# Hybrid decoder layer on one core: the small stores of the softmax statistics move from SP's queue to POOL's

## The chip, the cores and the metric

The kernel runs on one NeuronCore of a Trainium2 chip. The core has a matmul engine (PE), a vector engine (DVE), an activation engine (ACT), a general engine (POOL) and a sequencer that here only issues DMA transfers (SP). Each engine works through its own list of instructions in order; semaphores tie the lists together. The metric is device time in microseconds for one launch, the median of several runs.

## The reference

One layer of a decoder trunk, sequence 2048, width 1024, float32. After an RMS norm and one input projection, four mixers of 256 channels run side by side; their gated outputs are concatenated, projected, normed and added to the input. The change touches mixer A, softmax attention with three dilated windows, whose outputs are mixed by their softmax denominators:

```python
def _dilated_branch(q, k, v, window, dil, slopes):
    ...
    scores = jnp.where(mask, scores + bias, -jnp.inf)
    m = jnp.max(scores, axis=-1, keepdims=True)
    p = jnp.exp(scores - m)
    den = jnp.sum(p, axis=-1, keepdims=True)
    o = jnp.einsum('bhrnqk,bhrnkd->bhrnqd', (p / den).astype(v.dtype), vc)
    lse = (m + jnp.log(den))[..., 0]
    ...

def _dilated_mixture(q, k, v):
    slopes = _alibi_slopes(q.shape[1])
    outs, lses = [], []
    for window, dil in DILATED_PAIRS:          # ((128, 1), (512, 4), (2048, 16))
        o, lse = _dilated_branch(q, k, v, window, dil, slopes)
        outs.append(o)
        lses.append(lse)
    w = jax.nn.softmax(jnp.stack(lses), axis=0)
    o = jnp.einsum('gbhs,gbhsd->bhsd', w.astype(v.dtype), jnp.stack(outs))
    ...
```

There are four heads of 64 channels, 2048 queries each. Mixers B (spatial gating), C (pooling) and D (retention) are computed earlier and are not touched.

## The kernel before

Matmul operands are split into a high and a low part of float32r, so that one product is several matmuls.

**Stages.** First come the projections and the mixers B, C and D, in two halves of the sequence; they leave q, k, v and the gates in device memory (`qk`, `vd`, `agd`, `yb`). Then follows attention, head by head: heads 0 and 1 in `attention(0)`, 2 and 3 in `attention(1)`. Each head runs its branches in the order of dilation 4, 16, 1. A branch has 16 blocks of 128 queries, so a head has 48 blocks and the stage 192. For each block PE makes scores (`ps_s`), DVE adds the bias and takes the maximum (`att_p`, L639), ACT the exponential (L641), PE transposes (`ps_pt`), ACT and DVE split (L648, L649), PE multiplies by the values (`ps_o`), and ACT and DVE add the two halves into `att_o` (L663, L664).

**The loads of a head** are q2 (L565, L566), k2a (L568), k2b (L569) and three sets of values `att_v` (L578, L581, L576). They share seven buffers with the reordered queries `q2b` (L589 on DVE and POOL, L591 on DVE), so that each load waits until the last reader of an earlier tile is done.

**The statistics.** Each branch leaves maximum and denominator of its queries in `att_st`, 128 x 2 x 16. `keep_stats` transposes them on PE (`ps_st`), copies them on DVE to `sT` (L724, one buffer for all branches) and stores `sT` to `std` in device memory in the order of the sequence: eight stores of 2 KB for dilation 4 (L732), two for dilation 16 (L735), one for dilation 1 (L726). They are 40 stores and 4 more over the stage. `weigh` loads a head's three branches back (`sv`, L740), works out the weights on DVE (L742 to L752) and stores them to `fd` (L753).

**Combining.** `combine(0)` takes heads 0 and 1 in eight chunks of 256 queries, and has two buffers, so the chunks go in pairs. A chunk loads the weights `fb` (L763) and the gate `sga` (L765); POOL multiplies two branches (L766, L767), DVE the third (L768), adds (L769, L770) and gates (L772); ACT and POOL split the result (L776, L777), and SP stores it (L779). It has no place of its own in time: it runs among the blocks of heads 2 and 3. `combine(1)` follows the last head.

**Partial and final output.** Nine of the 16 output tiles get the products of mixers B, C and D during attention (`partial`: load `yraw` L785, split on POOL L797 and L798, matmuls `ps_out`, store `partd` L818). `final` adds attention's part, norms and stores.

**Order.** The code is not run in the order in which it is written: a scheduler orders the instructions of each engine ahead of time, by its own estimate of when each will be ready. Before the change SP issues every DMA. A DMA takes one of eight completion semaphores in turn, so it also waits for the DMA eight places before it.

Of the kernel before, what the change touches and what calls it, by code (L numbers as in the profile page):

```python
# [85 lines left out]
def hymba(ctx: ExitStack, tc: tile.TileContext, x, pre_g, w_in, sgu_g, sgu_w, sgu_b, pool_w,  # L86
          pool_scale, ret_g, w_out, post_g, cmix, catt, out, dbg=None, npart=9, spread=(0.3, 0.95)):
    nc = tc.nc
    V, A, G, T, D = nc.vector, nc.scalar, nc.gpsimd, nc.tensor, nc.sync
# [7 lines left out]
    def transpose(o, i, n=P):  # L97
        T.transpose(o, i, ident[:n, :n])  # L98
# [456 lines left out]
    def attention(p, tab):  # L555
        o01 = (big if p == 0 else po).tile([P, 2, SEQ], F32, tag="big" if p == 0 else "o01", name="att_o01")
        o = [o01[:, 0], o01[:, 1], po.tile([P, SEQ], F32, tag="o2", name="att_o2")]
        for s in range(2):
# [11 lines left out]
            for b, dil in enumerate(DILS):  # L570
                vt = pm.tile([P, 16, 2 * HD], F32R, tag="m8", bufs=7, name="att_v")
                dst = r32(vt)
                if dil == 1:
                    src = v_d[h].rearrange("(n t c) d -> c t n d", c=4, t=32)
                    for c in range(4):
                        D.dma_start(dst[c * 32:(c + 1) * 32], src[c])  # L576
                elif dil == 4:
                    D.dma_start(dst.rearrange("q (j c) d -> q j (c d)", j=4),  # L578
                                v_d[h].rearrange("(j q c) d -> q j (c d)", j=4, c=4))
                else:  # L580
                    D.dma_start(dst.rearrange("q r d -> q (r d)"), v_d[h].rearrange("(q r) d -> q (r d)", r=16))  # L581
                qb = q2
                if dil != 1:
                    qb = pm.tile([P, SEQ], F32R, tag="m8", bufs=7, name="q2b")
                    if dil == 4:
                        src = r32(q2).rearrange("p (j k c i) -> p c j k i", j=4, c=4, i=8)
                        dst = qb.rearrange("p (j c k i) -> p c j k i", j=4, c=4, i=8)
                        for c in range(4):
                            (V if c < 3 else G).tensor_copy(dst[:, c], src[:, c])  # L589
                    else:  # L590
                        V.tensor_copy(qb.rearrange("p (r w i) -> p r w i", r=16, i=8),  # L591
                                      r32(q2).rearrange("p (w r i) -> p r w i", r=16, i=8))
                st = p2.tile([P, 2, 16], F32, tag="stat", bufs=2, name="att_st")
                branch(h, dil, qb, k2a, k2b, vt, tab, o[b], st)
                keep_stats(h, b, dil, st)
# [123 lines left out]
    def keep_stats(h, b, dil, st):  # L719

        pt = ps2.tile([P, GRP], F32, tag="t", bufs=N_T, name="ps_st")
        transpose(pt[:32, :P], st.rearrange("p z n -> p (z n)"))
        sT = p2.tile([32, P], F32, tag="sT", bufs=1, name="sT")
        V.tensor_copy(sT, pt[:32, :P])  # L724
        if dil == 1:
            D.dma_start(st_d[h][b].rearrange("z (n q) -> (z n) q", q=P), sT)  # L726
            return
        for z in range(2):
            dst, src = st_d[h][b, z], sT[z * 16:(z + 1) * 16]
            if dil == 4:  # L730
                for j in range(4):
                    D.dma_start(dst.rearrange("(j k c i) -> j c k i", j=4, k=16, c=4)[j],  # L732
                                src[j * 4:j * 4 + 4].rearrange("c (k i) -> c k i", i=8))
            else:
                D.dma_start(dst.rearrange("(w r i) -> r w i", r=16, i=8), src.rearrange("r (w i) -> r w i", i=8))  # L735

    def weigh(h):

# [175 lines left out]
```

## Time and profile before

| | |
|---|---|
| median of 3 runs | 1062.74 us (1060.38 to 1069.5) |
| profiled execution, its time | 1066.84 us |
| its span, first to last instruction | 1065.1 us |
| its mean granted TensorE clock | 0.973 |
| PE busy | 993.5 us, 93% |
| DVE, ACT, POOL busy | 51%, 36%, 18% |
| DMA | 135.27 MB, 119962 packets |

The profile is one execution. A share of busy time is an average over stages with different limits. A row of a timeline has the start in us, the duration, the engine (SPq is SP's list of DMA issues), the line in the kernel, the operation, what it writes and reads, how many instructions were merged and, in brackets, how long the engine had stood idle before it and what ended that. A row of a group has busy time, mean duration in ns, then the idle time before its instructions and what ended it.

### The profile page before, as it was taken

To read this page: it belongs to the slowest core of one execution; us is meant where nothing else is said; L and a number is where in the kernel's file an instruction comes from. 1 tells how busy PE (TensorE), PEld (TensorE's weight loads), DVE (VectorE), ACT (ScalarE), POOL (GpSimd) and SP (SyncE) were. 2 spreads that over 40 slices of the span, in tenths; PEclk is the share of its full clock that TensorE was granted. 3 is DMA by queue.
4 is the path that set the end of the run, shared out by engine and by line. 5 is a ranking of instruction groups with operands and counts; after the bars stand their busy time and mean duration, and the time that the engine had idled before them with its cause. 6 is when DMAs were issued, how large, how long until landed. Compare 5 with 4: busy or idle time off the path is not lost. (4 is left out here: it accounts for less than half of the span.)

```text
span 1065.1 us, 15690 instructions
## 1 busy us (share of the span) xinstructions
PE 993.5 (93%) x5916; PEld 855.0 (80%) x5916; DVE 540.4 (51%) x1547; ACT 379.6 (36%) x851; POOL 190.9 (18%) x195
## 2 busy tenths in 40 slices
PE   5899999999999999999999999979998779988993
PEld 5888898988877988989898787778988569867872
DVE  7611216696332422023763321287776677547898
ACT  6320222131222421122211121498877448513231
POOL 2310012211232000002210134031122351142000
PEclk9999999999999999999999999998999879989997
DMA  8530313233223331042211830395659953484776
GB/s 279 147 99 20 100 60 114 85 120 92 86 79 99 99 100 39 25 135 80 80 41 50 210 119 20 116 213 162 147 168 201 207 152 85 109 270 129 268 259 217
DMA packets 119962, 135.27 MB, mean 127 GB/s; under 512 B 14928, under 2 KB 95952, under 8 KB 117840
## 3 DMA queue, kind: packets, MB, share of 16 engines
q1 hardware_dynamic: 119888, 134.29, 43.6%
q8 instruction: 46, 0.75, 0.3%
q14 instruction: 28, 0.23, 0.1%
HBM read 97.80 MB, written 36.47 MB: 126 GB/s over the span
## 5 line engine op out<-in xcount | busy, mean ns | idle before, releaser
L95 PE MATMUL ps_t<-hh,w 128*128 128x512 f32 x1152 | 370.1, 398 | 2.3 <-DVE b_t L370 2.3
L95 PEld LDWEIGHTS ps_t<-hh,w 128*128 128x128 f32 x1152 | 216.7, 189 | 52.4 <-issue 3.4
L95 PE MATMUL ps_t<-hl,w 128*128 128x512 f32 x576 | 227.6, 395 | 0.0
L95 PE MATMUL ps_m<-w,hh 128*128 128x256 f32 x1024 | 183.8, 282 | 2.0 <-ACT hh L230 1.6
L95 PE MATMUL ps_out<-wo,yt 128*128 128x512 f32 x576 | 155.6, 414 | 6.1 <-DVE yt L798 3.1
L95 PEld LDWEIGHTS ps_m<-w,hh 128*128 128x128 f32 x1024 | 157.5, 190 | 3.9 <-ACT hh L230 2.8
L95 PE MATMUL ps_m<-w,hl 128*128 128x256 f32 x512 | 145.4, 284 | 0.2 <-DVE hl L231 0.2
L95 PEld LDWEIGHTS ps_out<-wo,yt 128*128 128x128 f32 x576 | 109.8, 198 | 31.1 <-DVE yt L798 4.4
L95 PEld LDWEIGHTS ps_t<-hl,w 128*128 128x128 f32 x576 | 108.7, 189 | 24.3 <-issue 1.4
L250 DVE TENSOR_TENSOR w<-raw,w 128x1024 fp32r<-128x1024 f32 x42 | 59.0, 1412 | 109.6 <-ACT w L248 109.4
L95 PEld LDWEIGHTS ps_m<-w,hl 128*128 128x128 f32 x512 | 97.6, 191 | 0.8 <-DVE hl L231 0.4
L641 ACT ACTIVATE att_p<-att_p,att_st 128x128 f32<-128x128 f32 (+1 forms) x192 | 86.4, 453 | 20.5 <-DVE att_st L639 20.0
L248 ACT ACTIVATE w<-raw 128x1024 fp32r<-128x1024 f32 (+1 forms) x56 | 55.0, 997 | 70.1 <-PE ps_t L95 37.6
L639 DVE CUSTOM_DVE_ANT_0 att_p<-ps_s,tab 128x128 f32<-128x128 f32 (+1 forms) x192 | 60.3, 357 | 34.5 <-PE ps_s L95 31.0
L95 PE MATMUL ps_o<-pt_hi,att_v 128*128 128x128 f32 (+1 forms) x204 | 54.4, 287 | 6.2 <-DVE att_o L664 4.2
L649 DVE TENSOR_TENSOR pt_lo<-ps_pt,pt_hi 128x512 fp32r<-128x512 f32 x80 | 51.2, 650 | 12.5 <-ACT pt_hi L648 12.1
L95 PE MATMUL ps_o<-pt_lo,att_v 128*128 128x128 f32 (+1 forms) x204 | 52.8, 294 | 3.5 <-DVE pt_lo L649 3.4
L98 PE MATMUL ps_pt<-ident,att_p 128*128 128x128 f32 x300 | 51.2, 283 | 0.8 <-ACT att_p L641 0.8
L95 PEld LDWEIGHTS ps_o<-pt_hi,att_v 128*128 128x128 f32 x204 | 40.8, 200 | 9.5 <-DVE att_o L664 4.6
L648 ACT ACTIVATE pt_hi<-ps_pt 128x512 fp32r<-128x512 f32 x80 | 44.1, 563 | 11.2 <-PE ps_pt L98 5.7
L95 PE MATMUL ps_s<-k2a,q2b 128*128 128x128 f32 (+1 forms) x128 | 37.5, 325 | 8.6 <-DMA k2a<-qk 4.4
L95 PEld LDWEIGHTS ps_o<-pt_lo,att_v 128*128 128x128 f32 x204 | 40.6, 199 | 5.9 <-DVE pt_lo L649 4.8
(160 smaller groups left out, 1319.8 us busy)
## 6 DMA issues: line engine op xcount, KB each, us to landing
raw<-in_w_in_dram SPq DMA_DIRECT2D x52, 512.0 KB
qk<-qk_s SPq DMA_DIRECT2D x16, 512.0 KB
att_v<-vd SPq DMA_DIRECT2D x8, 1024.0 KB
xr<-in_x_dram SPq DMA_DIRECT2D x16, 512.0 KB
out_dram<-z SPq DMA_DIRECT2D x15, 512.0 KB
xt<-in_x_dram SPq DMA_DIRECT2D x7, 1024.0 KB
yraw<-yb SPq DMA_DIRECT2D x16, 384.0 KB
partd<-z SPq DMA_DIRECT2D x9, 512.0 KB
```

The costliest lines, as they stand in the source:

```text
L95: return T.matmul(o, lhsT, rhs, start=start, stop=stop, skip_group_check=True)
L98: T.transpose(o, i, ident[:n, :n])
L248: A.activation(hi, raw[:, :, cs], AF.Copy, scale=sc)
L250: eng.tensor_tensor(lo, raw[:, :, cs], r32(hi), ALU.subtract)
L639: V.tensor_tensor_reduce(out=pr[:, u, :w], in0=ps[:, u, :w], in1=bb, scale=-SLOPES[h] * HD ** -0.5, scalar=3e38, op0=ALU.add, op1=ALU.min, ...
L641: A.activation(pr[:, u, :w], pr[:, u, :w], AF.Exp, bias=neg, scale=-1.0, accum_out=st[:, 1, n:n + 1])
L648: A.activation(hi, pt[:, :w], AF.Copy)
L649: V.tensor_tensor(lo, pt[:, :w], r32(hi), ALU.subtract)
```

## The change

The stores of the two dilated branches (L732 and L735) are issued by POOL instead of SP. The store of dilation 1 (L726) stays with SP. The data, their places and their sizes are the same.

```diff
             dst, src = st_d[h][b, z], sT[z * 16:(z + 1) * 16]
             if dil == 4:
                 for j in range(4):
-                    D.dma_start(dst.rearrange("(j k c i) -> j c k i", j=4, k=16, c=4)[j],
+                    G.dma_start(dst.rearrange("(j k c i) -> j c k i", j=4, k=16, c=4)[j],
                                 src[j * 4:j * 4 + 4].rearrange("c (k i) -> c k i", i=8))
             else:
-                D.dma_start(dst.rearrange("(w r i) -> r w i", r=16, i=8), src.rearrange("r (w i) -> r w i", i=8))
+                G.dma_start(dst.rearrange("(w r i) -> r w i", r=16, i=8), src.rearrange("r (w i) -> r w i", i=8))
```

`D` is SP, `G` is POOL. The scheduler makes a new order from it, on every engine, from the end of head 0 on. Three places matter here.

SP where head 1's loads are issued (`q_6493` is head 1's q2, `std_82` head 0's statistics); a row with - stood there before, one with + stands there now:

```order
 L566 DMA q_6493<-qk_66 64x2048
 L548 DMA wo_raw<-in_w_out_dram 128x1024 x2
-L732 DMA std_82<-sT 4x16x8 x8
 L568 DMA k2a<-qk_68 64x2048 x2
-L735 DMA std_82<-sT 16x16x8 x2
 L569 DMA k2b<-qk_68 64x2048 x2
 L578 DMA att_v<-vd 128x4x512
```

The ten stores no longer stand before k2a and k2b. On POOL they stand between the two products of a weight split (L550) and head 1's quarter of `q2b` (L589).

POOL where the first pair of chunks of heads 0 and 1 is combined, while head 2 runs (`std_84` is head 2's statistics, `att_o_5880` and `att_o_5881` the outputs of heads 0 and 1). Before:

```order
L766 TENSOR_TENSOR fb<-fb,att_o_5880 128x256
L767 TENSOR_TENSOR fb<-fb,att_o_5881 128x256
L797 CAST yt<-yraw 128x3x128
L777 TENSOR_TENSOR ysa<-fb,ysa 128x256 x2
L798 TENSOR_TENSOR yt<-yraw,yt 128x3x128
```

And now:

```order
L766 TENSOR_TENSOR fb<-fb,att_o_5880 128x256
L767 TENSOR_TENSOR fb<-fb,att_o_5881 128x256
L797 CAST yt<-yraw 128x3x128
L732 DMA std_84<-sT 4x16x8 x8
L798 TENSOR_TENSOR yt<-yraw,yt 128x3x128
L777 TENSOR_TENSOR ysa<-fb,ysa 128x256 x2
L797 CAST yt<-yraw 128x3x128
L735 DMA std_84<-sT 16x16x8 x2
L798 TENSOR_TENSOR yt<-yraw,yt 128x3x128
```

Eight stores and one L798 have come between the products and L777, and two stores ahead of the next pair. On DVE, 22 score blocks (L639) now stand between L772 of the first pair and L768 of the second, where 8 stood. The three pieces of head 3's `q2b` (L589), which stood in the third pair, now stand in the second.

DVE at the fourth pair, where head 3 begins its values (`att_o_7252` is head 2's output, whose L664 frees a bank for `ps_o`). Before, the pair and the weights of head 2 (L742 to L745) were mixed with L664:

```order
L768 TENSOR_TENSOR fb<-fb,att_o_5880 128x256
L742 TENSOR_TENSOR nm<-sv 128x16
L772 TENSOR_TENSOR fb<-fb,sga 128x2x16x8
L769 TENSOR_TENSOR fb<-fb 128x256
L743 TENSOR_TENSOR nm<-nm,sv 128x16
L664 TENSOR_TENSOR att_o_7252<-ps_o,att_o_7252 64x512
L770 TENSOR_TENSOR fb<-fb 128x256
L745 TENSOR_TENSOR df<-sv,nm 128x48
```

Now L664 follows the whole pair, and the weights precede it:

```order
L752 TENSOR_TENSOR ew<-ew,nm 128x48
L768 TENSOR_TENSOR fb<-fb,att_o_5880 128x256 x2
L769 TENSOR_TENSOR fb<-fb 128x256
L770 TENSOR_TENSOR fb<-fb 128x256
L772 TENSOR_TENSOR fb<-fb,sga 128x2x16x8
L769 TENSOR_TENSOR fb<-fb 128x256
L770 TENSOR_TENSOR fb<-fb 128x256
L772 TENSOR_TENSOR fb<-fb,sga 128x2x16x8
L664 TENSOR_TENSOR att_o_7252<-ps_o,att_o_7252 64x512 x2
```

On PE, 18 `ps_out` now stand ahead of head 3's first `ps_o` where none stood; between that `ps_o` and the last `ps_st` of head 3 there are 19 more than before, and so 37 fewer partial products behind the last `ps_st`. On SP, the last `partd` store and the last two `wo_raw` loads now come before the second `combine` loads its weights of head 3.

## The prediction

> **What bounds the kernel now.** I read the page's head and busy shares first, then the windows, then the timelines of the engines where the small stores stand.
>
> ```profile
> span 1065.1 us, 15690 instructions
> PE 993.5 (93%) x5916; PEld 855.0 (80%) x5916; DVE 540.4 (51%) x1547; ACT 379.6 (36%) x851; POOL 190.9 (18%) x195
> q1 hardware_dynamic: 119888, 134.29, 43.6%
> 450.00:500.00 50.00, 50.00 (x332) 44.12 (x331) 13.56 (x20) 12.24 (x14) 7.58 (x6) 1.00 0.33 103
> 715.00:720.00 5.00, 2.40 (x12) 2.43 (x13) 2.48 (x5) 4.70 (x17) 0.00 (x0) 0.66 1.07 225
> 720.00:725.00 5.00, 3.13 (x15) 2.76 (x15) 1.28 (x6) 3.48 (x7) 0.00 (x0) 0.50 0.83 241
> 850.00:855.00 5.00, 1.84 (x6) 1.12 (x6) 4.02 (x10) 1.29 (x5) 3.98 (x5) 0.50 0.95 377
> ```
>
> A window row gives the stretch, its length, the busy time of PE, PEld, DVE, ACT and POOL, the granted clock, the DMA share and GB/s. The projections fill PE wholly (the row at 450 us), and nothing of the change stands there. The attention stage, from 683 us, has holes on PE: at 715 us, where head 1 begins, and around 850 us, where heads 0 and 1 are combined. In both the granted clock falls to 0.50. So the change is judged at these two places and at what follows them. The data of all DMA goes through one queue, q1, which is SP's; POOL issues none.
>
> **Head 1's start.** On SP the stores stand in front of the loads of the next head (start, duration, issue, count).
>
> ```profile
> L732 SPq DMA_DIRECT2D std<-sT x32: 241/317/855, 702.4 to 896.6; - x32
> 702.41 7.61 SPq L732 DMA_DIRECT2D std<-sT  x8
> 710.12 1.09 SPq L568 DMA_DIRECT2D k2a<-qk  x2
> 712.74 1.09 SPq L569 DMA_DIRECT2D k2b<-qk  x2
> 756.10 9.12 SPq L732 DMA_DIRECT2D std<-sT  x8
> 768.92 0.81 SPq L735 DMA_DIRECT2D std<-sT  x2
> 894.06 2.81 SPq L732 DMA_DIRECT2D std<-sT  x8
> 903.55 1.13 SPq L735 DMA_DIRECT2D std<-sT  x2
> 701.68 0.27 PE L95 MATMUL ps_o<-pt_lo,att_v 128*128 128x128 f32 x1
> 711.69 0.28 PE L95 MATMUL ps_s<-k2b,q 128*128 128x256 f32 x1
> 717.60 0.77 PE L95 MATMUL ps_s<-k2a,q2b 128*128 128x128 f32 x2 [4.42 <-DMA k2a<-qk]
> 722.71 0.44 PE L95 MATMUL ps_s<-k2b,q2b 128*128 128x128 f32 x1 [1.87 <-DMA k2b<-qk]
> ```
>
> Eight L732 stores hold SP for 7.61 us, 0.95 us each, though one issue's median is 0.317 us. Behind them wait k2a and k2b, 1 MB each. I infer that k2a takes the buffer of head 0's first values, last read at 701.68, and k2b one whose last scores run at 711.69. With the stores gone, k2a can go out at about 702 and land by 710, from its own 7.5 us (710.12 to 717.60). k2b is held by PE's read more than by SP: it goes out at about 711.9 instead of 712.74. Its 10 us to landing had k2a ahead in the queue; alone, 1 MB at the window's 225 GB/s is 4.4 us, and with some 2.8 us for issue and latency (estimate, the landing of a small store below) it lands at 719 instead of 722.7. That is 3.7 us. PE meanwhile works through its k2a part and eight ps_o, so its hole is short, and I count 1.3 us for the half-speed clock after it: **-5 us**.
>
> POOL could undo it: its L735 waits for the second transpose sT, and its quarter of q2b (L589) for head 1 stands behind L735.
>
> ```profile
> 696.73 4.75 POOL L550 TENSOR_TENSOR wo<-wo_raw,wo 128x1024 fp32r<-128x1024 f32 x2 [0.60 <-ACT wo L549]
> 711.53 0.28 DVE L724 COPY sT<-ps_st 32x128 f32<-32x128 f32 x1 [0.56 <-PE ps_o L95]
> 712.04 0.61 POOL L589 CAST q2b<-q 128x512 fp32r<-128x512 f32 x1 [10.55 <-PE ps_s L95]
> 786.71 2.78 DMA std<-sT
> ```
>
> **The unknown price** is what one store costs POOL, since no row shows POOL issuing a DMA. From below, an issue on SP, 0.32 us; an instruction that POOL did not have can give it nothing back, so below nothing is excluded. From above, POOL's longest row, L550, 4.75 us for two, so 2.4 us. I take 0.95 us, the pace of these very stores at 702.41, the nearest row.
>
> The Trainium skill, "DMA: Bandwidth & Descriptors", section "Anatomy of one DMA — SWDGE (gpsimd) path", fits about 2.0 us for each DMA on POOL's path, most of it completion and not setup. Were all of the 2.0 us POOL's own time, the sum would end some 30 us higher; if only the setup is, it stands. No run before the change shows which.
>
> At 0.95 us, POOL's eight end at 710 and have landed at 712.8 (2.78 us, the row of L726's store). DVE's second sT copy needs that, as sT has one buffer: DVE stands about 1 us, and all behind it on DVE too. L735 then ends at 715 and L589 at 716, ahead of k2b at 719, which hides them; from 1.4 us a store on it does not. Further on, the stores of the two branches are 12.8 us apart in head 1 (756.10 to 768.92) and 9.5 in head 3; the eight need 7.6 + 2.8 = 10.4, so DVE waits 1 us in head 3. I leave these 2 us inside the roundings.
>
> **The combining of heads 0 and 1** is a chain of four pairs of chunks, each begun by its fb loads.
>
> ```profile
> L768 DVE TENSOR_TENSOR fb<-fb,att_o 128x256 f32<-128x256 f32 x8 | 4.2, 530 | 17.6 <-DMA fb<-fd 17.6
> 810.00 0.42 DVE L768 TENSOR_TENSOR fb<-fb,att_o 128x256 f32<-128x256 f32 x1 [4.85 <-DMA fb<-fd]
> 828.07 0.43 DVE L768 TENSOR_TENSOR fb<-fb,att_o 128x256 f32<-128x256 f32 x1 [3.80 <-DMA fb<-fd]
> 846.21 0.43 DVE L768 TENSOR_TENSOR fb<-fb,att_o 128x256 f32<-128x256 f32 x1 [4.97 <-DMA fb<-fd]
> 866.09 0.43 DVE L768 TENSOR_TENSOR fb<-fb,att_o 128x256 f32<-128x256 f32 x1 [2.84 <-DMA fb<-fd]
> 872.11 0.68 DVE L664 TENSOR_TENSOR att_o<-ps_o,att_o 64x512 f32<-64x512 f32 x1
> 874.90 0.57 DVE L772 TENSOR_TENSOR fb<-fb,sga 128x256 f32<-128x256 f32 x1
> 818.16 0.27 DVE L639 CUSTOM_DVE_ANT_0 att_p<-ps_s,tab 128x128 f32<-128x128 f32 x1
> 823.85 0.41 DVE L639 CUSTOM_DVE_ANT_0 att_p<-ps_s,tab 128x256 f32<-128x256 f32 x1
> 817.92 1.70 POOL L777 TENSOR_TENSOR ysa<-fb,ysa 128x256 fp32r<-128x256 f32 x2 [0.34 <-ACT ysa L776]
> 820.76 3.33 SPq L763 DMA_DIRECT2D fb<-fd  x3
> 842.21 1.17 SPq L578 DMA_DIRECT2D att_v<-vd  x1
> 864.90 4.48 PE L95 MATMUL ps_out<-wo,yt 128*128 128x512 f32 x18 [0.57 <-ACT z L817]
> ```
>
> The pairs begin at 810, 828, 846 and 866 us. DVE stands at the head of each until fb lands, 17.6 us over the stage, and the last product ends at 875.5. In the new order POOL has head 2's eight L732 and an L798 between the products and L777 of pair 1. L777 feeds SP's L779, behind which stand three fb loads, k2b and the values of head 3. The eight cost 7.6 and the L798 1.0 us, so L777 comes at 826.5 instead of 817.9. SP is then otherwise idle, and its three loads, 3.33 us here among q2's and k2a's transfers, should land some 2.5 us sooner: **pair 2** at 834. That wait is filled: 22 score blocks now stand between L772 of pair 1 and L768 of pair 2 where 8 stood, and those 8 (818.16 to 823.85) took 6 us, so 22 take 17. Head 2's two L735, at the head of POOL's products, add 1.9. **Pair 3** follows after 18.1 us as before and 2 us for the three q2b copies that moved into pair 2: 856. Pair 3 then needs 16 us, not 19.9, since the head 3 values that went out at 842 (from 842.21, 2 MB) no longer meet its loads: **pair 4** at 872 to 873, its end at 879. DVE's L664, which frees the bank for head 3's first ps_o, stood inside pair 4 and now stands behind it: 880.5 instead of 872.1, **+8 us**.
>
> **Head 3 and the tail.** In PE's new order 18 ps_out stand ahead of that ps_o, hidden in its wait. 19 more than before stand between it and the last ps_st; at 4.48/18 = 0.25 us, **+4.7 us**. All 37 used to follow the last ps_st.
>
> ```profile
> 920.42 0.11 PE ps_st L98
> 935.86 10.48 DMA partd<-z
> 930.00:940.00 10.00, 7.13 (x21) 5.07 (x21) 2.87 (x2) 2.37 (x4) 2.36 (x1) 0.75 1.05 314
> 1050.00:1060.00 10.00, 0.00 (x0) 0.00 (x0) 9.79 (x31) 1.89 (x5) 0.00 (x0) 0.56 0.55 210
> ```
>
> So PE has 37 x 0.25 = 9.2 us less in the tail. But the tail begins with the second combine, whose fb loads stood behind the last partd store, and ends on DVE, with no matmul after 1050. The last partd and wo_raw, 1 MB, now go out ahead of it, 3.3 us at 314 GB/s. I take **-4 us**, between 0 (the chain alone decides) and -9.2 (PE alone).
>
> **Sum**, against the profiled execution: -5 + 8 + 4.7 - 4 = +3.7 us on 1066.84, of which its span is 1065.1. The median of the runs, 1062.74, lies 0.4% under that execution; I put the same difference on the median: 1066.5 us.
>
> **Rivals.**
>
> *POOL pays much more per store* (slower). For: POOL's plain instructions take 0.5 to 2.4 us. Against: it is busy 18% and could spare the time elsewhere. The point is 1.3 us a store. At 1.6 us: pair 2 another 5.2 us late; head 1's eight landed at 718, L589 done at 722, so 4.5 of the -5 us go; DVE's second copies wait 2.8 more in head 1 and 6 in head 3: 1066.5 + 18.5 = 1085. At 2.4 us, some 1110.
>
> *SP's relief is worth more than POOL's delay* (faster). At 0.32 us a store L777 slips by 3.6, not 8.6 (-5). If the blocks ahead of pair 2 also save its 3.80 us stall (-4) and the tail follows PE (-5), it is 1052. For: all 17.6 us of stalls end on fb loads that SP issues. Against: the chain is serial, and work that fills a wait does not shorten it.
>
> *No more than a new order*: the stores cost neither queue anything that shows, and the same matmuls run in another order. 1063, inside the forecast's own range.
>
> **How the numbers follow.** Forecast, with the third case in it: 0.49 (1057 to 1075). POOL's price: 0.30, half of it over 1085. SP's relief: 0.21. This kernel's measurement cannot tell less than 1%, 1052 to 1073, from no change. Faster 0.19, nearly all from the relief; slower 0.31, the price and the forecast's edge; same 0.50. The range, 1049 to 1086, takes in the relief and a price up to 1.6 us, and leaves the dearer half of the price out.
>
> **What will show it.** 40 issues by POOL, whose spacing is the price: 0.95 us. k2a out at 702, head 1's first k2b scores at 719. L777 of pair 1 some 9 us behind its L776. The last product of pair 4 at 874 to 880, the last ps_st at about 928, then a shorter tail. I am wrong if POOL spends over 1.3 us a store, if DVE's second sT copies stand over 2 us, or if the tail shrinks by the full 9 us.

## The result and the profile after

The changed kernel takes 1072.67 us (median of 9 runs, 1068.69 to 1076.88), the kernel before, run beside it, 1064.10 us (9 runs). The ratio is 1.0072, 95% interval 1.0049 to 1.0095: slower by 0.7%, where the forecast had 0.35%, inside its range and its case of "no change". (A ratio with its interval is worked out from all runs of both kernels; it is not the quotient of the two medians, which here is 1.0081.) Its profiled execution took 1068.69 us.

First the page of the changed kernel: span, busy times, then the DMA queues with packets, MB and share of 16 engines.

```profile
span 1067.0 us, 15740 instructions
PE 989.6 (93%) x5916; PEld 852.5 (80%) x5916; DVE 537.3 (50%) x1547; ACT 379.9 (36%) x851; POOL 212.0 (20%) x235
q1 hardware_dynamic: 115536, 134.16, 43.5%
q0 software_dynamic: 1280, 0.16, 0.2%
```

POOL now has a queue of its own, q0, with 40 more instructions and 21 us more busy time. PE has the same 5916 matmuls, and its busy time is 3.9 us less; what grew is its idle time.

The two profiled executions can't be laid over each other by their clocks. The last L331 on ACT ends the stage ahead of attention; here are its rows, of before, then of after.

```profile
683.42 1.10 ACT L331 ACTIVATE ag_s<-ps_t 128x512 f32<-128x512 f32 x1 [4.31 <-PE ps_t L95]
679.01 1.10 ACT L331 ACTIVATE ag_s<-ps_t 128x512 f32<-128x512 f32 x1 [4.31 <-PE ps_t L95]
```

The execution of before came there 4.41 us later, in a stage that the change does not touch. All positions below are therefore counted from this row in each kernel's own trace ("at 28.1" is 28.1 us behind it). From there before needs 381.7 us to its end and after 388.0: **+6.3**, while the spans differ by 1.9.

**Head 1's start.** Timelines of SP, POOL, DVE and PE after, then POOL's issues of a store and the time from issue to landing of all transfers of `std`, then the DMA share (the column ahead of the GB/s) by 5 us. The last three rows are what SP waited for ahead of k2a, the time to landing of k2a's two halves, and PE's first scores on k2b.

```profile
701.10 1.09 SPq L568 DMA_DIRECT2D k2a<-qk  x2
707.50 1.09 SPq L569 DMA_DIRECT2D k2b<-qk  x2
698.30 5.07 POOL L732 DMA_DIRECT2D std<-sT  x8 [1.24 <-DVE sT L724]
712.67 0.28 DVE L724 COPY sT<-ps_st 32x128 f32<-32x128 f32 x1 [5.49 <-DMA std<-sT]
713.01 1.11 PE L98 MATMUL ps_pt<-ident,att_p 128*128 128x128 f32 x4 [4.98 <-DVE sT L724]
715.34 0.80 PE L95 MATMUL ps_s<-k2a,q2b 128*128 128x128 f32 x2 [1.22 <-DVE q2b L589]
L732 POOL DMA_DIRECT2D std<-sT x32: 620/622/770, 698.3 to 903.3; - x32
DMA to landing us min/median/max: 1.4/5.1/10.6
701.00:706.00 5.00, 3.75 (x31) 3.26 (x30) 3.95 (x13) 4.93 (x18) 2.37 (x4) 1.00 1.05 279
706.00:711.00 5.00, 2.02 (x16) 1.78 (x16) 1.18 (x5) 4.93 (x19) 0.00 (x0) 0.96 1.05 203
SPq L568 <- PE ps_pt L98: 4.0, 1, 4.0
DMA to landing us min/median/max: 9.8/10.7/11.6
719.10 0.46 PE L95 MATMUL ps_s<-k2b,q2b 128*128 128x128 f32 x1
```

k2a leaves at 22.1, where before has 26.7. The forecast was 702, which is 18.6 from the L331 row; SP, free of the stores, still waits 4.0 us for PE there. k2a's second half, issued at 22.6, lands 11.6 us later, at 34.2: no sooner than in before, where PE's wait for k2a ends at 34.2 (717.60). On top of that POOL's stores, all issued by 703.4, hold DVE's second sT copy until 712.67; DVE stands 5.49 us, PE behind it 4.98, and the first scores on k2a run at 36.3 (before: 34.2), those on k2b at 40.1 (before: 39.3). By the third sT copy the kernels are level (54.57 after, 54.60 before).

**Combining and tail.** DVE's wait at the head of each of the four pairs, then POOL, SP, DVE's L664, the last sT copy and the start of the second combine.

```profile
L768 DVE TENSOR_TENSOR fb<-fb,att_o 128x256 f32<-128x256 f32 x8 | 4.4, 552 | 18.5 <-DMA fb<-fd 18.5
829.63 0.42 DVE L768 TENSOR_TENSOR fb<-fb,att_o 128x256 f32<-128x256 f32 x1 [3.83 <-DMA fb<-fd]
854.36 0.43 DVE L768 TENSOR_TENSOR fb<-fb,att_o 128x256 f32<-128x256 f32 x1 [3.22 <-DMA fb<-fd]
870.84 0.42 DVE L768 TENSOR_TENSOR fb<-fb,att_o 128x256 f32<-128x256 f32 x1 [4.69 <-DMA fb<-fd]
814.66 1.43 POOL L777 TENSOR_TENSOR ysa<-fb,ysa 128x256 fp32r<-128x256 f32 x2
817.56 5.87 SPq L763 DMA_DIRECT2D fb<-fd  x3
877.85 1.26 DVE L664 TENSOR_TENSOR att_o<-ps_o,att_o 64x512 f32<-64x512 f32 x2
929.20 0.28 DVE L724 COPY sT<-ps_st 32x128 f32<-32x128 f32 x1
951.66 0.69 DVE L768 TENSOR_TENSOR fb<-fb,att_o 128x512 f32<-128x512 f32 x1 [14.87 <-DMA fb<-fd]
820.00:840.00 20.00, 10.21 (x63) 8.11 (x62) 11.36 (x31) 10.19 (x31) 6.17 (x8) 0.84 1.00 233
```

L777 of pair 1 is hardly late (135.7 against 134.5), yet pair 2 is 6 us late, in a stretch where the DMA engines are full (share 1.00) and PE works 10 of 20 us. (In the same stretch of before, 824.41 to 844.41, the share is 0.93 and PE works 17.2 us.) Pairs 3 and 4 are 12.6 and 9.2 late, the last sT copy 13.0. Then the tail gives 6.7 back.

### The profile page after: what moved, and what is told of

Same layout as the page of the kernel before. It is cut to its first block, busy times and chain, and to the rows that moved or that the text cites. A ratio compares the mean times of both kernels' runs of the same rounds, so it can differ in the third digit from the quotient of the medians.

```text
span 1067.0 us, 15740 instructions
## 1 busy us (share of the span) xinstructions
PE 989.6 (93%) x5916; PEld 852.5 (80%) x5916; DVE 537.3 (50%) x1547; ACT 379.9 (36%) x851; POOL 212.0 (20%) x235
## 3 DMA queue, kind: packets, MB, share of 16 engines
q1 hardware_dynamic: 115536, 134.16, 43.5%
q0 software_dynamic: 1280, 0.16, 0.2%
## 4 chain that ended last, share of the span: by engine, by line
PE 75%; DMA 12%; DVE 6%; issue 3%; POOL 1%; ACT 1%; SPq 1%; DVEq 0%; POOLq 0%; ACTq 0%
PE ps_t L95 38%; PE ps_m L95 15%; PE ps_out L95 9%; DMA fb<-fd 4%; PE ps_o L95 3%; PE ps_s L95 2%; PE ps_pt L98 2%; PE ps_of L95 2%; DMA cm<-in_cmix_dram 1%; DMA std<-sT 1%; DMA out_dram<-z 1%; PE ps_in L95 1%; DMA raw<-in_w_in_dram 1%; DVE z L850 1%; PE ps_mix L95 1%
## 5 line engine op out<-in xcount | busy, mean ns | idle before, releaser
L95 PE MATMUL ps_out<-wo,yt 128*128 128x512 f32 x576 | 152.4, 409 | 8.2 <-POOL yt L798 5.8
L95 PE MATMUL ps_m<-w,hl 128*128 128x256 f32 x512 | 145.3, 284 | 0.0
L641 ACT ACTIVATE att_p<-att_p,att_st 128x128 f32<-128x128 f32 (+1 forms) x192 | 86.6, 454 | 32.1 <-DVE att_st L639 31.5
L639 DVE CUSTOM_DVE_ANT_0 att_p<-ps_s,tab 128x128 f32<-128x128 f32 (+1 forms) x192 | 60.6, 358 | 33.1 <-PE ps_s L95 27.8
L649 DVE TENSOR_TENSOR pt_lo<-ps_pt,pt_hi 128x512 fp32r<-128x512 f32 x80 | 51.6, 651 | 13.0 <-ACT pt_hi L648 10.6
L444 POOL TENSOR_TENSOR d_g<-d_g,ret_b 128x512 f32<-128x512 f32 x8 | 10.3, 1287 | 181.4 <-ACT d_g L442 181.4
L648 ACT ACTIVATE pt_hi<-ps_pt 128x512 fp32r<-128x512 f32 x80 | 44.3, 564 | 5.4 <-PE ps_o L95 2.8
L98 PEld LDWEIGHTS ps_pt<-ident,att_p 128*128 128x128 f32 x300 | 34.7, 144 | 13.2 <-DVE sT L724 6.1
```

What stands on the lines that cost most here:

```text
L95: return T.matmul(o, lhsT, rhs, start=start, stop=stop, skip_group_check=True)
L444: G.tensor_tensor(o, o, ret_b.unsqueeze(1).broadcast_to([P, 2, 256]), ALU.mult)
L639: V.tensor_tensor_reduce(out=pr[:, u, :w], in0=ps[:, u, :w], in1=bb, scale=-SLOPES[h] * HD ** -0.5, scalar=3e38, op0=ALU.add, op1=ALU.min, ...
L641: A.activation(pr[:, u, :w], pr[:, u, :w], AF.Exp, bias=neg, scale=-1.0, accum_out=st[:, 1, n:n + 1])
L648: A.activation(hi, pt[:, :w], AF.Copy)
L649: V.tensor_tensor(lo, pt[:, :w], r32(hi), ALU.subtract)
```

## The experiments

The change does two things: the stores go through another queue, and the scheduler, which foresees that, orders PE, DVE, ACT and POOL anew. **My theory** after the first reading was that POOL's late landings eat the relief at head 1; **the rival**, that the new order alone makes the loss. To part them, the experiments fix the order: each engine's instructions are chained in a listed order (issue order only, no wait added).

```diff
     with tile.TileContext(nc, schedule_with_timeline_sim=True) as tc:
         hymba(tc, *args)
+        pin(tc, nc)      # the order of before, of the change, or one up to a point and then the other
```

| kernel | stores by | order | median us | ratio to before, 95% interval |
|---|---|---|---|---|
| the change | POOL | new | 1072.67 | 1.0072 (1.0049 to 1.0095) |
| order alone | SP | new | 1072.58 | 1.0102 (1.0077 to 1.0127) |
| POOL, old order | POOL | before | 1064.84 | 1.0036 (1.0014 to 1.0059) |
| POOL, two sT | POOL | new | 1069.75 | 1.0083 (1.0061 to 1.0105) |
| POOL, old order, two sT | POOL | before | 1063.56 | 1.0013 (0.9995 to 1.0032) |
| new, then old | SP | new to the end of combining | 1072.53 | 1.0081 (1.0056 to 1.0107) |
| old, then new | SP | new from there on | 1071.08 | 1.0071 (1.0049 to 1.0093) |
| one plain store | SP | before | 1059.99 | 0.9969 (0.9950 to 0.9988) |
| ACT | ACT | before | 1075.74 | 1.0123 (1.0100 to 1.0146) |
| k2a first, two sT | SP | before, k2a ahead of the stores | 1060.17 | 0.9993 (0.9970 to 1.0015) |
| POOL, one plain store | POOL | before | 1061.06 | 1.0005 (0.9981 to 1.0028) |
| q first | SP | new, q and k2a ahead | 1071.97 | 1.0101 (1.0067 to 1.0134) |
| q first, stores behind | SP | same, stores held back too | 1075.27 | 1.0120 (1.0095 to 1.0146) |

Each ratio is to the kernel before on the same chip, whose medians lay between 1061.62 and 1064.10. Positions in the profiled executions, in us from the L331 row, each read from the timeline of that kernel:

| kernel | head 0's 2nd sT copy | its 3rd | pair 2 | pair 4 | head 3's first sT copy | its last | end |
|---|---|---|---|---|---|---|---|
| before | 28.1 | 54.6 | 144.7 | 182.7 | 210.3 | 237.2 | 381.7 |
| the change | 33.7 | 54.6 | 150.6 | 191.8 | 219.4 | 250.2 | 388.0 |
| order alone | 28.1 | 54.6 | 152.3 | 195.2 | 221.3 | 252.1 | 389.5 |
| POOL, old order | 36.1 | 57.7 | 148.5 | 188.2 | 213.6 | 240.4 | 380.9 |
| POOL, old order, two sT | 28.2 | 56.2 | 146.6 | 187.0 | 214.9 | 241.8 | 385.2 |
| new, then old | 28.7 | 55.3 | 151.4 | 193.4 | 221.2 | 248.0 | 390.3 |
| old, then new | 28.2 | 54.9 | 145.3 | 184.0 | 217.5 | 248.3 | 390.4 |
| one plain store | 28.3 | 53.5 | 142.8 | 181.2 | 208.9 | 235.7 | 379.6 |
| k2a first, two sT | 27.5 | 51.5 | 143.1 | 180.9 | 207.8 | 234.6 | 375.9 |

These are single executions, and executions of one kernel differ by some 11 us (before: 1056.02 to 1066.89 in one series); the verdicts come from the medians, the table says where. Near its start the table is steadier than that: in the six runs whose stores and loads at head 1 stand as in before, the second sT copy runs at 28.1 to 28.7 and the third at 54.1 to 55.3. One thing sets the four pinned runs with stores on POOL apart: in each of their profiled executions the granted clock fell to half for 3.4 us, 3.5 to 4.0 us behind the L331 row and ahead of the first store. Here are the windows from 4 to 7 us behind that row, of POOL, old order, two sT, and of before; the clock is the column ahead of the DMA share.

```profile
682.35:685.35 3.00, 3.00 (x17) 3.00 (x15) 1.42 (x8) 3.00 (x12) 0.00 (x0) 0.50 0.99 320
687.42:690.42 3.00, 2.88 (x25) 2.55 (x23) 2.32 (x12) 3.00 (x13) 0.00 (x0) 1.00 0.89 274
```

So these four come to head 0's first sT copy some 1.4 us late (20.0 to 20.1, elsewhere 18.7), and that much of their positions is not the stores' doing. The change itself has no such dip. Why they have it, and whether their unprofiled runs do, is not known.

**Order against queue.** The order alone, stores kept on SP:

> All stores stay on SP, at the places they have before (head 0's: eight ahead of k2a, two ahead of k2b); PE, DVE, ACT and POOL follow the changed kernel's order row for row, and SP its order for the rest. ORDER THEORY (the loss comes from the new order around the combining of heads 0 and 1): it is slower than before like the change itself, 1071 to 1075 us, since it has the order's loss and no relief at head 1. QUEUE THEORY (the loss comes from what POOL's queue does to the stores, late landings and the sT wait of 5.49 us): 1062 to 1066, as before. DVE's second sT copy of head 0 waits under 1 us in both.

POOL's queue in the order of before:

> The 40 stores go through POOL's queue as in the change, but PE, DVE, ACT, POOL and SP follow the order of before row for row (on POOL the stores are put in, on SP they are left out). ORDER THEORY: no slower than before, 1060 to 1066: the relief of SP at head 1 (4.4 us for k2a and k2b) and the sT wait of 5.5 us cancel there, and nothing is lost in the combining. QUEUE THEORY: 1070 to 1075 as in the change, with pair 2's fb loads landing late again although POOL's products stand where they stood.

The order alone is as slow as the change, though DVE has no stall there at the second sT copy. POOL's queue in the old order costs 0.36%, a third of it, more than the order theory allowed, though its median, 1064.84, lies in that theory's span. So the loss is mainly the order's; the queue adds at most some 6 us in the old order (upper end 0.59%, and the early dip of the clock may be part of it), and in the new order nothing that shows, since the intervals of the change and of the order alone overlap.

**The sT wait.** Two buffers instead of one.

```diff
-        sT = p2.tile([32, P], F32, tag="sT", bufs=1, name="sT")
+        sT = p2.tile([32, P], F32, tag="sT", bufs=2, name="sT")
...
-        sv = p2.tile([P, 3, 2, 16], F32, tag="sv", bufs=2, name="sv")
+        sv = p2.tile([P, 3, 2, 16], F32, tag="sv", bufs=1, name="sv")
```

> The change in its own order, row for row, with two buffers for sT (and one for sv, to make room), so that the second sT copy of a head no longer waits for the first one's stores. LANDING THEORY (the 5.49 us that DVE stands at head 0's second sT copy eat the relief): that wait goes, head 1 starts about 5 us sooner against the start of the attention stage, and the time is 1066 to 1069. RIVAL (PE would stand for k2b there anyway, or the gain is lost again at the combining, which waits for its own loads): the wait goes and the time stays at 1071 to 1074.

> POOL's queue for the stores, the order of before, and two sT buffers. If both the order theory and the landing theory hold: 1056 to 1061, faster than before by the 5 us of head 1. If only the order matters: 1060 to 1066. If POOL's queue itself is the loss beyond the sT wait: 1067 or more.

DVE's wait goes in both, and no gain shows: 1.0083 in the new order, where one buffer had 1.0072, and 1.0013 in the old, where one buffer had 1.0036 (the intervals overlap both times). The median of the new order, 1069.75, lies between the spans of the landing theory and its rival, but in the profile another wait stands behind, as the rival had it. It is k2a itself; here SP and PE of POOL, old order, two sT.

```profile
701.81 1.09 SPq L568 DMA_DIRECT2D k2a<-qk  x2
714.63 0.77 PE L95 MATMUL ps_s<-k2a,q2b 128*128 128x128 f32 x2 [6.35 <-DMA k2a<-qk]
```

From issue to scores k2a now takes 12.8 us; before it took 7.5 (710.12 to 717.60). Sent 3.2 us sooner, at 23.5 instead of 26.7, it is used 2.1 later, at 36.3 (the dip of the clock has its part in that).

**How much relief there is.** One plain store of sT for eight, and one for two, so that SP has next to nothing to issue. This kernel leaves out the reordering of the statistics and serves for its time alone:

```diff
-        for z in range(2):
...
+        D.dma_start(st_d[h][b].rearrange("z (n q) -> (z n) q", q=P), sT)
```

> The order of before, and in place of eight L732 or two L735 one plain store of the whole sT on SP, in the place of the first of them. The statistics so lie in DRAM as they stand in sT, not put in the order of the sequence, so the branches are weighted by wrong rows; the number, the place and the waits of all other work are unchanged. It bounds from above what any other queue can give. RELIEF THEORY (SP's 7.6 us for the eight held the loads back, as the prediction's -5 had it): 1054 to 1058. RIVAL (the DMA engines are full when head 1 begins, and k2a sent sooner lands no sooner): 1060 to 1064, with k2a out some 7 us sooner and the first scores on q2b at most 2 us sooner against the start of the attention stage.

And with the stores left as they are, but behind k2a:

> The order of before, all stores on SP as they are, two sT buffers, but in heads 0 and 1 the two k2a loads of the next head go ahead of the eight L732: k2a, four L732, k2b, four L732, two L735. It gives the loads the relief that POOL's queue was to give, with no second queue. If the plain-store run's gain (k2a out at 22 after the start of the stage, its scores at 31.5 where before has 34.2) was the relief of SP alone: 1060 to 1062 us beside 1063 of before. If the gain came from fewer small pieces in the DMA engines, k2a's scores run at 34 or later and the time is that of before, 1062 to 1066.

SP and PE, one plain store first, then k2a first:

```profile
701.94 1.09 SPq L568 DMA_DIRECT2D k2a<-qk  x2
711.39 0.47 PE L95 MATMUL ps_s<-k2a,q2b 128*128 128x128 f32 x2 [1.55 <-DMA k2a<-qk]
703.00 1.09 SPq L568 DMA_DIRECT2D k2a<-qk  x2
704.18 1.54 SPq L732 DMA_DIRECT2D std<-sT  x4
710.55 2.19 SPq L732 DMA_DIRECT2D std<-sT  x4
711.88 0.30 PE L95 MATMUL ps_s<-k2a,q2b 128*128 128x128 f32 x1 [1.51 <-DMA k2a<-qk]
717.16 0.45 PE L95 MATMUL ps_s<-k2b,q2b 128*128 128x128 f32 x1 [2.86 <-DMA k2b<-qk]
```

The plain store is worth 3.3 us over the whole kernel (0.31%, 0.12 to 0.50). That is taken as the bound of what any queue can win in this order, and is short of the relief theory's 1054 to 1058; the rival had the time, though k2a left 4.6 us sooner, not 7, and its scores run 2.7 us sooner, not 2. With k2a first, its scores run at 31.0 instead of 34.2, those on k2b at 36.2 instead of 39.3, and head 0 ends 3.1 us sooner in the profile. So the relief is real at its place, but the medians, 1060.17 beside 1061.62, don't tell it from nothing. The clock differs there too: from 30 to 50 us behind the L331 row it is 0.83 in this run, 0.74 in before and 0.66 in the plain-store run, whose head 0 ends only 1.1 us sooner. In these two runs and in the change k2a leaves at 22.1; with the stores on SP its scores run at 31.0 and 31.5, beside POOL's eight stores it lands at 34.2.

The windows of before suggest why it is not 5 us:

```profile
705.00:710.00 5.00, 4.10 (x34) 3.60 (x32) 3.94 (x16) 4.93 (x19) 0.00 (x0) 1.00 0.60 196
710.00:715.00 5.00, 2.80 (x20) 2.26 (x20) 4.40 (x18) 4.95 (x18) 0.61 (x1) 1.00 0.75 169
```

While SP stood, the DMA engines still worked off what had been sent, at 0.60 and 0.75. The idle rest, 0.40 x 5 + 0.25 x 5 = 3.3 us of transfer time, is an estimate of what can be won by sending sooner. It is no more than that, since a share of busy time is not a rate: 0.60 goes with 196 GB/s here, 1.05 with 203 in the change.

**Which queue.** POOL with the plain store, and ACT with the small ones:

> As the run with one plain store (statistics stored as they stand in sT, so the branches are weighted by wrong rows), but POOL issues these eight stores, two per head, in the order of before. SMALL PIECES THEORY (the 32-byte pieces of the stores, not POOL's queue, made them land late and kept k2a back): a store lands in about 3 us, k2a's scores run at 31 to 32 us after the start of the stage and the time is 1058 to 1061. SOFTWARE QUEUE THEORY: stores land in 6 us or more behind the large loads, DVE's second sT copy of head 0 waits 3 us or more, k2a's scores run at 34 to 36, 1062 to 1065.

> The order of before, with the 40 stores issued by ACT, so by a hardware queue as on SP. SOFTWARE QUEUE THEORY (POOL's descriptors are what lands late): ACT's stores land within about 3 us, DVE's second sT copy of head 0 waits under 1 us, and the time is 1060 to 1063, or higher by what the issues cost ACT. FULL ENGINES THEORY (any store sent behind the large loads lands late when it is not behind them on one queue): landings of 5 to 10 us and an sT wait of 4 us or more there, 1064 to 1068.

POOL's rows of "POOL, one plain store" and the landing of its eight stores, then k2a's issue and scores:

```profile
L728 POOL DMA_DIRECT2D std<-sT x8: 502/513/659, 700.8 to 901.8; - x8
std<-sT POOLq DMA_DIRECT2D x8, 16.0 KB, 6.2
703.57 1.09 SPq L568 DMA_DIRECT2D k2a<-qk  x2
715.01 0.77 PE L95 MATMUL ps_s<-k2a,q2b 128*128 128x128 f32 x2 [4.59 <-DMA k2a<-qk]
```

The answer is mixed. As the software-queue theory had it, the median landing is 6.2 us, and k2a is 11.4 us under way, where beside the same plain stores on SP it was 9.5 (701.94 to 711.39). Against it, DVE waits only 0.4 us and the time is that of before. On SP's queue, too, a transfer of `std` in the plain-store run took up to 10.4 us to land, so lateness is not POOL's alone. Why k2a is 2 us longer under way beside a single store on POOL's queue was not settled.

ACT, whose list is full here (4.9 of 5 us busy in the windows above), is the wrong place; its issues and PE's row behind them:

```profile
702.54 5.10 ACTq L732 DMA_DIRECT2D std<-sT  x3
709.24 0.47 PE L95 MATMUL ps_o<-pt_hi,att_v 128*128 128x128 f32 x1 [6.30 <-ACT pt_hi L648]
```

The last three of eight issues take it 5.10 us, and PE stands 6.30 us for the L648 behind them. The kernel as a whole is 1.23% slower. What ACT's issues waited for is not shown, the landings of its stores are not in the trace, and the sT copy was late for another reason, so neither theory is borne out; what was measured is the price of stores in ACT's list, their waits included.

**Where in the order.** The new order up to the end of combining, then the old; and the reverse.

> All stores on SP. Every engine follows the changed kernel's order up to the end of the combining of heads 0 and 1 (on PE up to the last ps_out ahead of head 3's scores in the third branch of head 2), and the order of before from there. COMBINING THEORY (the loss arises among the four pairs): 1070 to 1074 us, with pair 2's L768 at 148 to 153 us after the start of the attention stage, where before has 144.65, and the last pair's at 192 to 197, where it has 186.6. TAIL THEORY (it arises in head 3, by the ps_out ahead of its last ps_st): 1061 to 1065.

> The other half: all stores on SP, the order of before up to the end of the combining, the changed kernel's from there. COMBINING THEORY: 1058 to 1063, no slower than before and perhaps faster, since head 3 and the tail in the new order gave 3 us back after the combining (aligned, the change stood +13 at head 3's last sT and +6.3 at the end). TAIL THEORY: 1067 to 1073.

Each theory is right on the half that it blames and wrong on the other: both halves lose, 0.81% and 0.71%, and together hardly more (1.02%). The first half makes L664 late, which frees the bank of head 3's first ps_o; the second puts 18 ps_out ahead of that ps_o. PE in "new, then old", then DVE and PE in "old, then new":

```profile
881.23 0.48 PE L95 MATMUL ps_o<-pt_hi,att_v 128*128 128x128 f32 x1 [11.23 <-DVE att_o L664]
869.19 0.68 DVE L664 TENSOR_TENSOR att_o<-ps_o,att_o 64x512 f32<-64x512 f32 x1
872.47 5.87 PE L95 MATMUL ps_out<-wo,yt 128*128 128x512 f32 x18 [4.28 <-ACT z L817]
878.18 0.22 PE L95 MATMUL ps_o<-pt_hi,att_v 128*128 128x128 f32 x1
```

Alone, the first leaves PE idle for 11.23 us. Alone, the second has the bank free at 869.19 and PE at ps_o only at 878.18, behind the 18 ps_out (5.87 us) and their own wait (4.28). Together, the ps_out run in the hole.

**Why pair 2 is late in the new order.** q and k2a of head 3 (2 MB) leave just ahead of pair 2's fb loads there, and were to be sent sooner:

> The order of the change with all stores on SP, as in the order-alone run, but SP sends q and k2a of head 3 (2 MB) right behind pair 1's fb loads, ahead of the two sga loads and the stores, and so some 5 us sooner, where before has them. LOADS THEORY (pair 2 comes late because its fb loads meet these 2 MB, sent only when sga's buffer was free): pair 2's L768 at 146 to 148 us after the start of the stage instead of 152.3, and the time 3 to 6 us under the order-alone run: 1067 to 1070. BLOCKS THEORY (pair 2 comes late because 22 score blocks stand ahead of it on DVE): L768 stays at 150 to 153 and the time at 1071 to 1075.

> As the run before it, but now head 2's eight L732 are held behind q and k2a of head 3 on SP as well: there SP stood for the copy that those stores wait for, and q left only 2 us sooner, so nothing was told apart. LOADS THEORY: q and k2a leave at 120 to 128 us after the start of the stage, their 2 MB are through before pair 2's fb loads leave at 138, DVE's wait for these (6.5 us in the order-alone run) falls under 2 us, pair 2's L768 runs at 146 to 148, and the time is 1066 to 1069 us. BLOCKS THEORY (DVE reaches L768 late in any case): L768 at 150 or later, 1071 to 1075. If q's buffer is not free before 131, q leaves no sooner and the question stays open.

The first missed its aim: SP stood for the stores of head 2's first branch, and q left only 2 us sooner; no change (1.0101). In the second q waited at SP's head until its buffer was free:

```profile
811.55 0.47 SPq L565 DMA_DIRECT2D q<-qk  x1
827.72 1.94 SPq L763 DMA_DIRECT2D fb<-fd  x3
834.65 0.43 DVE L768 TENSOR_TENSOR fb<-fb,att_o 128x256 f32<-128x256 f32 x1 [6.69 <-DMA fb<-fd]
```

q left at 131.8 (before: 127.4), and with the stores in between the fb loads left some 8 us later than in the order-alone run. Still L768 came only 2.6 us later (154.9 against 152.3), which points to the full engines, more than the time of issue, as what sets the landing. That speaks for the transfers, while place and time (154.9, 1075.27 us) are those of the blocks theory; but q did not leave before 131, as this run needed, and the 2 MB were never moved out of the way, so how the 6 to 8 us divide between them and the 22 blocks stays open. DVE reached L768 at 145.8 in the order-alone run (152.3 less its wait of 6.47), so the transfers can account for at most those 6.5.

## Why the prediction was right, and where it was wrong

The time came out 6 us above the forecast, inside the range and the case of no change. By the steps, in the aligned profile:

- **Head 1's start, forecast -5, measured 0. This is the step that failed.** The forecast, in positions, had k2a out at 18.6 and landed by 26.6, from its own 7.5 us, and k2b, out at 28.5 with the engines to itself, landed at 35.6 instead of 39.3; these 3.7 us made most of the term. k2b left at 28.5 as said. But k2a left at 22.1, since SP had to wait for PE beyond the read at 701.68 that the forecast took for the last. From there it took 9 us to its scores with the stores behind it on SP (k2a first), and 12.1 to its landing beside POOL's stores, so that k2b met it under way and landed at 38.8. SP's side was nearly right in size: with k2a first, the scores on k2b came 3.1 us sooner. What failed is POOL's side. k2a landed no sooner than before, and DVE's stand at the second copy, put at about 1 us and left in the roundings, was 5.49, over the 2 us that the forecast had named as a sign of being wrong. In the three pinned runs with these small stores on POOL k2a takes 12.7 to 12.8 us to land; why it takes longer beside them is not shown.
- **POOL's price, 0.95 us taken, 0.62 measured** (0.57 for L735). The pace of the stores on SP was no issue price. Here are head 0's eight in the order-alone run, then what SP's stores waited for at head 1's start in before (us in total, times, longest).

```profile
697.50 1.79 SPq L732 DMA_DIRECT2D std<-sT  x5
700.81 4.09 SPq L732 DMA_DIRECT2D std<-sT  x3
SPq L732 <- DMA wo_raw<-in_w_out_dram: 3.1, 2, 2.3
SPq L732 <- DMA q<-qk: 2.0, 1, 2.0
```

  Five go at 0.36 us each, three at 1.36. In before, 5.1 of the 7.61 us are three waits for the landing of the loads eight places before (q2's second half, two of wo_raw). In head 3 of before, where no such wait shows, eight took 2.81 (894.06). POOL's eight go at some 0.62 each, the first at 0.77. So the first rival fell.
- **L777's slip, forecast 8.6, measured 1.2.** Pair 2, forecast 834, ran at 829.63, or 834.0 on before's clock: the right number, but not by this cause, since it is as late with all stores on SP. The pairs behind were 12.6 and 9.2 late, against 9.8 and about 6.4, and L664 10.2 late against 8. That the +8 came near is partly luck.
- **Head 3, +4.7 forecast:** from its first sT copy to the last, 4.0 were added. The 18 ps_out were hidden in the wait for L664, as said; with that cover gone, they cost.
- **The tail, -4, between 0 and -9.2:** -6.7 by the end, -5.1 by the start of the second combine (272.7 less 250.2, where before has 264.8 less 237.2), which its fb loads end after a 14.87 us wait. It did not shrink by PE's full 9.2.
- **The rivals.** SP's relief was 3.3 us in the plain-store run (at most 5.3 by its interval), not the 14 of its case. "No more than a new order" had the mechanism right and the size wrong: the order alone costs 0.8 to 1.3%.

The sum without the failed term is 8 + 4.7 - 4 = +8.7; the medians say +8.6. So close a fit is luck: the ratio's interval runs from 5.2 to 10.1 us, the aligned profile has +6.3, and the 8 rests in part on a slip of L777 that did not come. What the forecast had right is that the new order would lose more around the combining and in head 3 than the tail gives back, and the order-alone and half-order runs bear that out.

The Trainium skill, "DMA: Bandwidth & Descriptors", section "Issuing engines are not separate DMA queues", says that transfers begun by any engine share the same 16 DMA engines, and that issuing from several saves only issue time. The trace agrees: share 1.05 after the stores had their own queue, and k2a 12.1 us under way there. The Trainium skill, "Perfetto Trace Analysis", section "DMA Instruction — SWDGE (GPSIMD)", says that the end of such a row is the end of making descriptors, not of moving data; the 0.62 us row beside landings of up to 10.6 us agrees that the row's end is not the landing.

## What to carry to other kernels

Before a load is given an earlier start, read the DMA share where it would go: what the engines leave idle there is a first estimate of the gain. Before the pace of a queue's issues is taken as their price, read what the queue waited for. When a change makes a scheduler reorder, run the new order with the old resources and the old order with the new ones, since the two can have opposite causes and sizes. And measure the halves of an order together: work that fills a hole in one is a delay in the other.

## What was not expected of the hardware

- Eight stores of 2 KB behind large loads take the issuer about 0.36 us each for the first five and 1.4 for the last three on SP (1.7 on ACT), but 0.35 each in head 3. On SP the difference is waiting for the landing of earlier loads, 5.1 us in before; on ACT it is not shown.
- POOL's time for a store hardly depends on its shape: 0.62 us (2 KB), 0.57 (8 KB), 0.51 (16 KB plain). The same 40 stores are 4352 packets less on q1 (119888 to 115536) and 1280 on q0.
